# Stick-breaking attention: the triangular products of the suffix sums taken from two split parts of softplus

## The chip, the cores and the metric

One core of one Trainium2 chip runs the whole layer as one program. The metric is device time in microseconds (us), the median of three runs. Engines are named as in the profile: PE multiplies matrices (PEld is its weight load), DVE, ACT and POOL work on vectors, SP issues most of the DMAs.

## The reference

The layer has two attention groups side by side, an output projection, and a mixture of experts. The change is in the second group, stick-breaking attention, for 512 positions and 8 heads of 128 dimensions:

```python
def stick_breaking_block(q_blk, t_blk, k, v):
    s_pos = jnp.arange(k.shape[1], dtype=jnp.int32)
    strict = (s_pos[None, :] < t_blk[:, None])[None, None]
    z = jnp.einsum('bqhd,bshd->bhqs', q_blk, k).astype(jnp.float32)
    log_1m = jnp.where(strict, jax.nn.log_sigmoid(-z), 0.0)
    tail = lax.cumsum(log_1m, axis=3, reverse=True) - log_1m
    a = jnp.where(strict, jnp.exp(jax.nn.log_sigmoid(z) + tail), 0.0)
    return jnp.einsum('bhqs,bshd->bqhd', a.astype(v.dtype), v)
```

With log_sigmoid(-z) = -softplus(z) and log_sigmoid(z) = z - softplus(z), the weight of a position s is exp of z minus the sum of softplus over s and all later positions up to the query: a suffix sum of softplus along s.

## The kernel before

**Products.** Weights and activations of the big projections are held as two parts: a high part rounded to the type fp32r, and a low part, the float32 rest. Three products of 512 columns (`three`: high by high, high by low, low by high) replace one float32 product. In the attention stages the projections run as groups of six such products, named B (per-head projections, `main_b`) or Q (query projection, `main_q`) in the rows; these are the main products here. ACT rounds each weight chunk to its high part `hl`, and DVE subtracts to get the low part (`w_chunk`; POOL does it in a middle stretch).

**Stick-breaking.** The generator `stick(h)` does one head. Keys lie on the 128 partitions, queries on the free axis. Of each block of 128 keys only queries from that block on count, so the four key blocks have 512, 384, 256 and 128 columns. Three steps do them from the last keys to the first: blocks 3 and 2 together (256+128 = 384 columns), block 1 (384) and block 0 (512). Each step

- takes a PSUM bank `z` for the product of keys and queries (float32) and adds a strict causal mask;
- has ACT take |z|, exp and ln(1+...), and DVE (line 803) make softplus of it, in the tile `st` in SBUF, through the view `e`;
- adds onto `z`, on PE, the sums over all later key blocks (a product with `mones`, a matrix of minus ones, of the running column sums `tot`), and the suffix sum inside the block (a product with `negU`, which is the upper triangular matrix of ones minus one: only 0 and -1);
- keeps `tot` up to date on POOL;
- has ACT take exp of `z`, which gives the weights. `stick_pv` multiplies them with the values later.

The products with `mones` and `negU` are float32.

**What sets the order.** `tc.manual_schedule()` keeps the written order: each engine runs its instructions in the order in which the program issued them. Side work is written as generators in four lanes. `steps` runs the main products; after each group of six, `lanes.tick(rate)` advances lanes in turn, rate x 4 advances on average, and an advance runs a generator to its next `yield`. So what stands between two `yield` of `stick` is issued at once, and between one such piece and the next of the same head stand other lanes and, mostly, a group of main products. The rate is 1.2 (`RATES[0]`) while heads 0 to 3 run in two lanes, and 0.6 to 1.5 later. Heads 4 to 6 run at the same time in three lanes, head 7 behind them.

At the start of each main item `advance` issues the loads and the vector work of the weights: `w_chunk`, and `mod_chunk`, which sums the modulation's rows with one pass of DVE over 128x2048 per chunk (`gemv`, line 269, tile `accv`). These stand in DVE's queue between the passes of the heads. `norm_o` normalises group A beside the last blocks of heads 4 to 6: its passes are the rows Q, o00H, o00L, o01H and o01L.

**Pools.** Small tiles come from the pool `sm`, with rings by tag: "rb" has two buffers (among others the normalisation's `ro`), "tmp" three (`osq`, `rt`, `sqt`). A new tile of a ring waits until the tile that had its buffer has been read for the last time.

## Time and profile before

| | |
|---|---|
| median of three runs | 1876.78 us (1874.24 to 1879.22) |
| profiled execution, its own time | 1876.25 us |
| its span in the trace | 1874.4 us |
| mean granted clock of PE | 0.981 |
| busy: PE / DVE / ACT / POOL | 1735.2 / 938.9 / 507.6 / 153.2 us |
| stick-breaking's softplus passes on DVE | 24, between 248.8 and 668.5 us |

All times below come from the one profiled execution. A timeline row gives start, duration, engine, line, operation, what it writes and reads, and, in brackets, how long the engine was idle before it and what ended that. Ends of PE's products are modelled, so the start of the next product says more than a duration. A window row gives start and end, the length, the busy time of PE, PEld, DVE, ACT and POOL with their counts, the mean granted clock of PE, the DMA share and GB/s. Line 97 is the helper `act`, line 100 the helper `mm`, so go by tile names there. The mixture of experts, from about 700 us to the end, is bound by the DMAs of its weights.

### The profile page before, as it was taken

The page shows a single profiled execution, that of the slowest core. Times are in us where ns is not written, and L with a number is a line of the kernel's source. Part 1 is how long each engine was busy: PE and PEld are TensorE (multiplying, and loading weights), DVE is VectorE, ACT ScalarE, POOL GpSimd, SP SyncE. Part 2 cuts the span into 40 slices and gives each one's busy share as a digit, 9 for nine tenths or more (in the row PEclk, how much of TensorE's full clock was granted, in tenths as well). Part 3 has the DMA queues.
Part 4 walks back from the last instruction along what each step waited for, and adds up shares of the span by engine and source line. Part 5 has one row for each costly group of instructions (what it writes and reads, how often), then busy time and mean ns, then how long its engine had stood idle before and what let it go on. Part 6 is the DMA issues. An engine that isn't in the chain of part 4 may idle for free.

```text
span 1874.4 us, 20840 instructions
## 1 busy us (share of the span) xinstructions
PE 1735.2 (93%) x8097; PEld 975.6 (52%) x8097; DVE 938.9 (50%) x1518; ACT 507.6 (27%) x960; POOL 153.2 (8%) x116
## 2 busy tenths in 40 slices
PE   6999997999899998998899999999999999999997
PEld 3777775775567676887333333333333333333333
DVE  6798943378955857555334424342434233333425
ACT  4323342555455532321212111121112110211010
POOL 0001010332225110000100000000000000000000
PEclk8999998999999999999999999999999999999999
DMA  9876734312245645669899999999999999999997
GB/s 389 339 279 229 257 125 156 135 68 84 74 138 201 230 179 205 222 225 409 313 412 419 419 420 420 419 419 420 420 419 419 420 419 420 419 420 419 419 413 275
DMA packets 91574, 585.06 MB, mean 312 GB/s; under 512 B 10866, under 2 KB 11034, under 8 KB 27046
## 3 DMA queue, kind: packets, MB, share of 16 engines
q1 hardware_dynamic: 87184, 569.09, 76.0%
q0 software_dynamic: 4288, 14.60, 2.1%
q8 instruction: 65, 1.06, 0.2%
q14 instruction: 37, 0.30, 0.0%
HBM read 583.64 MB, written 8.40 MB: 316 GB/s over the span
## 4 chain that ended last, share of the span: by engine, by line
DMA 41%; PE 36%; DVE 14%; issue 4%; ACT 4%; POOL 1%; SPq 0%; DVEq 0%; ACTq 0%; POOLq 0%
DMA w_u<-in_w_up 15%; DMA w_g<-in_w_gate 12%; DMA w_d<-in_w_down 12%; PE O L100 8%; PE B L100 7%; PE y L100 3%; PE u L100 3%; PE Q L100 2%; PE g L100 2%; PE z L100 2%; DVE accv L269 2%; DVE acc L269 1%; PE cb L100 1%; DVE sel L722 1%; DMA w_m<-in_w_m 1%
## 5 line engine op out<-in xcount | busy, mean ns | idle before, releaser
L100 PE MATMUL u<-w_u,xe 128*64 128x512 f32 x1024 | 267.3, 605 | 22.8 <-DMA w_u<-in_w_up 21.6
L100 PE MATMUL g<-w_g,xe 128*64 128x512 f32 x1024 | 240.8, 596 | 18.2 <-DMA w_g<-in_w_gate 18.0
L1277 DVE TENSOR_TENSOR x<-cb,x 128x512 f32<-128x512 f32 x256 | 157.2, 681 | 186.2 <-PE cb L100 186.2
L100 PE MATMUL y<-w_d,uT 128*64 128x512 f32 x1024 | 236.9, 600 | 0.7 <-ACT uT L97 0.7
L100 PEld LDWEIGHTS u<-w_u,xe 128*64 128x64 f32 x1024 | 78.4, 138 | 200.9 <-issue 137.7
L100 PEld LDWEIGHTS g<-w_g,xe 128*64 128x64 f32 x1024 | 75.9, 137 | 170.5 <-issue 130.7
L269 DVE SCALAR_TENSOR_TENSOR accv<-w_m_None,sil,accv 128x2048 f32<-128x2048 f32 x62 | 150.4, 2426 | 6.7 <-DMA accv<-in_b_gate 6.5
L1267 DVE SCALAR_TENSOR_TENSOR yt<-y,gs,accv 128x512 f32<-128x512 f32 x64 | 47.8, 747 | 200.4 <-PE y L100 200.4
L97 ACT ACTIVATE xe<-ga,modc 128x128 f32<-128x128 f32 x254 | 93.9, 463 | 126.2 <-PE y L100 95.7
L100 PEld LDWEIGHTS y<-w_d,uT 128*64 128x64 f32 x1024 | 66.5, 136 | 116.0 <-issue 107.6
L100 PE MATMUL cb<-yH,oT 128*128 128x512 f32 x256 | 107.7, 421 | 0.9 <-DVE x L1277 0.9
L97 ACT ACTIVATE uT<-uT 128x512 f32<-128x512 f32 x16 | 9.6, 598 | 343.5 <-PE uT L1318 343.5
L100 PE MATMUL cb<-yL,oT 128*128 128x512 f32 x256 | 101.0, 394 | 0.0
L1269 DVE TENSOR_TENSOR yL<-yt,yH 128x512 fp32r<-128x512 f32 x64 | 44.3, 692 | 110.3 <-DMA w_g<-in_w_gate 52.7
L97 ACT ACTIVATE yH<-yt 128x512 fp32r<-128x512 f32 x64 | 40.3, 630 | 204.6 <-DVE yt L1267 121.4
L1219 POOL DMA_INDIRECT xg<-x1d,gi x15 | 15.2, 1014 | 818.7 <-DVE t L1222 597.2
L100 PEld LDWEIGHTS cb<-yH,oT 128*128 128x128 f32 x256 | 48.0, 188 | 49.8 <-issue 38.9
L1241 PEld LDWEIGHTS ga<-cst,xg 128*128 128x128 f32 x252 | 35.2, 209 | 62.9 <-issue 42.0
L97 ACT ACTIVATE hl<-w_B 128x1024 fp32r<-128x1024 f32 x48 | 50.5, 1052 | 54.9 <-DVE accv L269 29.5
L1312 DVE TENSOR_TENSOR u<-sg,u 128x512 f32<-128x512 f32 x16 | 11.0, 688 | 106.0 <-PE u L100 106.0
L381 DVE TENSOR_TENSOR hl<-w_O,hl 128x1024 fp32r<-128x1024 f32 x32 | 39.2, 1229 | 43.6 <-ACT hl L97 28.3
L381 POOL TENSOR_TENSOR hl<-w_B,hl 128x1024 fp32r<-128x1024 f32 x17 | 47.9, 2817 | 142.6 <-ACT hl L97 112.3
(428 smaller groups left out, 2915.4 us busy)
## 6 DMA issues: line engine op xcount, KB each, us to landing
w_g<-in_w_gate SPq DMA_DIRECT2D x128, 1024.0 KB, 19.9
w_u<-in_w_up SPq DMA_DIRECT2D x128, 1024.0 KB, 21.2
w_d<-in_w_down SPq DMA_DIRECT2D x128, 1024.0 KB, 19.9
w_m_None<-in_w_mod SPq DMA_DIRECT2D x64, 1024.0 KB, 4.9
w_m<-in_w_m SPq DMA_DIRECT2D x32, 1024.0 KB, 11.7
w_B<-in_w_b SPq DMA_DIRECT2D x48, 512.0 KB, 4.6
w_O<-in_w_o SPq DMA_DIRECT2D x16, 1024.0 KB, 5.0
w_A<-in_w_a SPq DMA_DIRECT2D x8, 848.0 KB, 11.3
```

The lines of the kernel that those rows point to most:

```text
L97: return SC.activation(o, i, f, **kw)
L100: return T.matmul(o, l, r, start=start, stop=stop, skip_group_check=skip)
L269: V.scalar_tensor_tensor(acc, w, s, acc, op0=OP.mult, op1=OP.add)
L381: low_eng[0].tensor_tensor(t[:, 1], s, t[:, 0].bitcast(F32), op=OP.subtract)
L722: V.match_replace(out=acc, in_to_replace=m8, in_values=acc, imm_value=SEL)
L1219: G.indirect_dma_start(xs, None, x1d[:, :], bass.IndirectOffsetOnAxis(ap=gi[:, 0:1], axis=0), bounds_check=S - 1, oob_is_err=False)
L1241: T.transpose(pb[:, 128 * j:128 * j + 128], xs[:, 512 * c:512 * c + 512].rearrange("p (k j) -> p j k", j=4)[:, j], ident)
L1267: V.scalar_tensor_tensor(yt, y, g, rowv[G2][:, cs], op0=OP.mult, op1=OP.mult)
L1269: V.tensor_tensor(yL[:, cs], yt, yH[:, cs].bitcast(F32), op=OP.subtract)
L1277: return lambda: V.tensor_tensor(acc[q][:, t], pb, acc[q][:, t], op=OP.add)
L1312: V.tensor_tensor(u, sg, pb, op=OP.mult)
```

## The change

`negU` gets the type fp32r; its values, 0 and -1, are the same in it. In each step of `stick` the products with `mones` stay as they were. Behind them two new tiles are made: `eH`, softplus rounded to fp32r by ACT, from the ring "rb"; and `eL` = softplus - eH, by DVE, from the ring "tmp". There is a `yield`; then `negU` is multiplied with eH and with eL, and the exponential is issued in the same piece. In the first step the addition on POOL is written ahead of the product with `mones`.

Per head that is three float32 steps of triangular products (four products, since the first step has two) replaced by eight products in fp32r, three more passes on ACT and three more on DVE. On ACT and DVE nothing else changes its place. `eL` is line 816, and lines behind it move by five.

```diff
@@ -132,7 +132,7 @@
     ones, mones = (t.to_broadcast([P, P]) for t in (one1, mone1))
     eps = sm.tile([P, 1], F32, name="eps")
     V.memset(eps, EPS)
-    negU = sm.tile([P, P], F32, name="negU")
+    negU = sm.tile([P, P], F32R, name="negU")
     cmask = cst[:, C_CM:C_CM + 128]
     ustrict = cst[:, C_US:C_US + 128]
     identb = sm.tile([P, P], BF, name="identb")
@@ -803,17 +803,22 @@
             V.scalar_tensor_tensor(e, z, 0.0, e, op0=OP.max, op1=OP.add)
             yield
             if js == (2, 3):
+                G.tensor_tensor(tot[:, 384:], e[:, 128:256], e[:, 256:384], op=OP.add)
                 mm(z[:, 128:256], mones, e[:, 256:384], False, False, True)
-                G.tensor_tensor(tot[:, 384:], e[:, 128:256], e[:, 256:384], op=OP.add)
             else:
                 mm(z[:, 128:], mones, tot[:, 128 * js[0] + 128:], False, False, True)
-            for j in js:
-                mm(z[:, at[j]], negU, e[:, at[j]], False, j == js[-1], True)
             if js == (1,):
                 G.tensor_tensor(tot[:, 256:], tot[:, 256:], e[:, 128:], op=OP.add)
             if js[0]:
                 G.tensor_copy(tot[:, 128 * js[0]:128 * js[0] + 128], e[:, 0:128])
-            yield
+            eH, eL = (sm.tile([P, S], F32R, name=n_, tag=t_, bufs=b_)[:, :n] for n_, t_, b_ in (("eH", "rb", 2), ("eL", "tmp", 3)))
+            act(eH, e)
+            V.tensor_tensor(eL, e, eH.bitcast(F32), op=OP.subtract)
+            yield
+            for j in js:
+                mm(z[:, at[j]], negU, eH[:, at[j]], False, False, True)
+            for j in js:
+                mm(z[:, at[j]], negU, eL[:, at[j]], False, j == js[-1], True)
             act(e, z, AF.Exp)
             yield
         weighed.append((h, buf))
```

DVE at head 3, middle and last block, before (`st<-z,st` is softplus, `accv` the modulation's sum, `hl` the low part of a weight chunk):

```order
L803 SCALAR_TENSOR_TENSOR st<-z,st 128x384
L269 SCALAR_TENSOR_TENSOR accv_2143<-w_m_None_2343,sil,accv_2143 128x2048
L381 TENSOR_TENSOR hl<-w_Q_2340,hl 128x1024
L803 SCALAR_TENSOR_TENSOR st<-z,st 128x512
L269 SCALAR_TENSOR_TENSOR accv_2143<-w_m_None_2408,sil,accv_2143 128x2048
L381 TENSOR_TENSOR hl<-w_Q_2450,hl 128x1024
```

The same place on DVE after the change:

```order
L803 SCALAR_TENSOR_TENSOR st<-z,st 128x384
L269 SCALAR_TENSOR_TENSOR accv_2184<-w_m_None_2391,sil,accv_2184 128x2048
L381 TENSOR_TENSOR hl<-w_Q_2388,hl 128x1024
L816 TENSOR_TENSOR eL<-st,eH 128x384
L803 SCALAR_TENSOR_TENSOR st<-z,st 128x512
L269 SCALAR_TENSOR_TENSOR accv_2184<-w_m_None_2458,sil,accv_2184 128x2048
L381 TENSOR_TENSOR hl<-w_Q_2504,hl 128x1024
L816 TENSOR_TENSOR eL<-st,eH 128x512
```

Each subtraction stands behind the modulation's pass and the weight split that follow the softplus it belongs to; nothing else moved.

PE at the middle block of head 3, before (Q is a main product):

```order
L100 MATMUL z<-st,mone_76 128x256
L100 MATMUL z<-st,negU 128x384
L100 MATMUL Q_2457<-cqsH,hl 128x512
L100 MATMUL Q_2457<-cqsL,hl 128x512
```

And after the change:

```order
L100 MATMUL z<-st,mone_76 128x256
L100 MATMUL z<-eH,negU 128x384
L100 MATMUL z<-eL,negU 128x384
L100 MATMUL Q_2511<-cqsH,hl 128x512
L100 MATMUL Q_2511<-cqsL,hl 128x512
```

Here the triangular products follow the sums without a main product between them, as before.

DVE at the first block of heads 4 to 6 (384 columns, three lanes), before:

```order
L803 SCALAR_TENSOR_TENSOR st<-z,st 128x384 x3
L267 TENSOR_SCALAR accv_4167<-w_m_None_4022,sil 128x2048
L269 SCALAR_TENSOR_TENSOR accv_4167<-w_m_None_4100,sil,accv_4167 128x2048
L381 TENSOR_TENSOR hl<-w_B_1_4103,hl 128x1024
L269 SCALAR_TENSOR_TENSOR accv_4167<-w_m_None_4165,sil,accv_4167 128x2048
L381 TENSOR_TENSOR hl<-w_B_1_4103,hl 128x1024
```

And after the change:

```order
L803 SCALAR_TENSOR_TENSOR st<-z,st 128x384 x3
L816 TENSOR_TENSOR eL<-st,eH 128x384 x2
L267 TENSOR_SCALAR accv_4235<-w_m_None_4086,sil 128x2048
L269 SCALAR_TENSOR_TENSOR accv_4235<-w_m_None_4164,sil,accv_4235 128x2048
L381 TENSOR_TENSOR hl<-w_B_1_4167,hl 128x1024
L816 TENSOR_TENSOR eL<-st,eH 128x384
L269 SCALAR_TENSOR_TENSOR accv_4235<-w_m_None_4233,sil,accv_4235 128x2048
L381 TENSOR_TENSOR hl<-w_B_1_4167,hl 128x1024
```

Two subtractions stand ahead of the two passes of the modulation and of the weight split, the third one behind them.

PE at the same block, second and third lane, before (B is a main product):

```order
L100 MATMUL z<-st,mone_76 128x128
L100 MATMUL z<-st,negU 128x256
L100 MATMUL z<-st,negU 128x128
L100 MATMUL z<-st,mone_76 128x128
L100 MATMUL z<-st,negU 128x256
L100 MATMUL z<-st,negU 128x128
L100 MATMUL B_4109<-hl,h0H 128x512 x2
L100 MATMUL B_4109<-hl,h0L 128x512
```

And after the change, where the triangular products of the first and of the second lane are seen:

```order
L100 MATMUL z<-st,mone_76 128x128
L100 MATMUL z<-eH,negU 128x256
L100 MATMUL z<-eH,negU 128x128
L100 MATMUL z<-eL,negU 128x256
L100 MATMUL z<-eL,negU 128x128
L100 MATMUL B_4174<-hl,h0H 128x512 x2
L100 MATMUL B_4174<-hl,h0L 128x512
L100 MATMUL B_4174<-hl,h0H 128x512 x2
L100 MATMUL B_4174<-hl,h0L 128x512
L100 MATMUL z<-eH,negU 128x256
L100 MATMUL z<-eH,negU 128x128
L100 MATMUL z<-eL,negU 128x256
```

The triangular products came directly behind their sums; now they follow a lane's advance later, with main products between, and a set is four products in place of two.

DVE at the last block of heads 4 to 6 (512 columns), before (Q and o01L are the normalisation):

```order
L803 SCALAR_TENSOR_TENSOR st<-z,st 128x512
L269 SCALAR_TENSOR_TENSOR accv_4167<-w_m_None_4294,sil,accv_4167 128x2048
L269 SCALAR_TENSOR_TENSOR accv_4167<-w_m_None_4349,sil,accv_4167 128x2048
L381 TENSOR_TENSOR hl<-w_B_3_4352,hl 128x1024
L888 SCALAR_TENSOR_TENSOR Q_2769<-Q_2769,vecs,ro_4307 128x512 x2
L892 TENSOR_TENSOR o01L<-Q_2769,o01H 128x512
L888 SCALAR_TENSOR_TENSOR Q_2769<-Q_2769,vecs,ro_4307 128x512
```

And after the change:

```order
L803 SCALAR_TENSOR_TENSOR st<-z,st 128x512
L816 TENSOR_TENSOR eL<-st,eH 128x512
L269 SCALAR_TENSOR_TENSOR accv_4235<-w_m_None_4382,sil,accv_4235 128x2048
L269 SCALAR_TENSOR_TENSOR accv_4235<-w_m_None_4446,sil,accv_4235 128x2048
L381 TENSOR_TENSOR hl<-w_B_3_4449,hl 128x1024
L816 TENSOR_TENSOR eL<-st,eH 128x512
L893 SCALAR_TENSOR_TENSOR Q_2833<-Q_2833,vecs,ro_4395 128x512 x2
L897 TENSOR_TENSOR o01L<-Q_2833,o01H 128x512
L893 SCALAR_TENSOR_TENSOR Q_2833<-Q_2833,vecs,ro_4395 128x512
L897 TENSOR_TENSOR o01L<-Q_2833,o01H 128x512
L816 TENSOR_TENSOR eL<-st,eH 128x512
```

The first lane's subtraction is ahead of the long passes, the second lane's behind them, and the third lane's five passes of the normalisation later.

PE at the same block, from the second lane's sums on, before:

```order
L100 MATMUL z<-st,mone_76 128x384
L100 MATMUL z<-st,negU 128x512
L100 MATMUL z<-st,mone_76 128x384
L100 MATMUL z<-st,negU 128x512
L100 MATMUL B_4110<-hl,h2H 128x512 x2
```

And after the change:

```order
L100 MATMUL z<-st,mone_76 128x384 x2
L100 MATMUL B_4174<-hl,h2H 128x512 x2
L100 MATMUL B_4174<-hl,h2L 128x512
L100 MATMUL B_4174<-hl,h2H 128x512 x2
L100 MATMUL B_4174<-hl,h2L 128x512
L100 MATMUL z<-eH,negU 128x512
L100 MATMUL z<-eL,negU 128x512
L100 MATMUL z<-eH,negU 128x512
L100 MATMUL z<-eL,negU 128x512
```

The sums of the second and the third lane now stand together, then a group of main products, and then the triangular products of the first two lanes.

## Rows read from the trace of the kernel before

**Rows 1.** The page: shares of the chain that ended last, by engine

```profile
DMA 41%; PE 36%; DVE 14%; issue 4%; ACT 4%; POOL 1%; SPq 0%; DVEq 0%; ACTq 0%; POOLq 0%
```

**Rows 2.** Windows: start:end, length, busy of PE, PEld, DVE, ACT, POOL, clock, DMA

```profile
330.00:370.00 40.00, 39.78 (x171) 28.98 (x171) 15.51 (x14) 22.28 (x38) 13.23 (x11) 1.00 0.40 140
...
395.00:440.00 45.00, 42.41 (x197) 30.04 (x195) 38.83 (x96) 24.60 (x57) 11.84 (x6) 0.96 0.21 71
```

**Rows 3.** Timeline of PE: start us, duration us, what, count

```profile
264.19 1.02 PE L100 MATMUL z<-B,B 128*128 128x512 f32 x2
...
265.05 0.22 PE L100 MATMUL z<-smaskb,identb 128*128 128x128 bf16 x1
...
598.26 5.49 PE B L100 x24
...
103.08 0.27 PE L100 MATMUL nat<-waH,h1H 128*128 128x208 f32 x1
...
103.19 0.27 PE L100 MATMUL nat<-waL,h1H 128*128 128x208 f32 x1
```

**Rows 4.** Groups of the page and of one tile (count: lowest/median/highest ns)

```profile
L1269 DVE TENSOR_TENSOR yL<-yt,yH 128x512 fp32r<-128x512 f32 x64 | 44.3, 692 | 110.3 <-DMA w_g<-in_w_gate 52.7
...
L97 ACT ACTIVATE yH<-yt 128x512 fp32r<-128x512 f32 x64 | 40.3, 630 | 204.6 <-DVE yt L1267 121.4
...
L97 ACT ACTIVATE st<-st x24: 523/526/632, 247.6 to 666.3; 128x384 f32<-128x384 f32 x16, 128x512 f32<-128x512 f32 x8
...
L803 DVE SCALAR_TENSOR_TENSOR st<-z,st x24: 547/558/693, 248.8 to 667.8; 128x384 f32<-128x384 f32 x16, 128x512 f32<-128x512 f32 x8
```

**Rows 5.** Timeline of DVE and PE, middle block of head 3

```profile
346.67 2.34 DVE L269 SCALAR_TENSOR_TENSOR accv<-w_m_None,sil,accv 128x2048 f32<-128x2048 f32 x1
...
346.90 0.67 PE L100 MATMUL z<-st,mone 128*128 128x256 f32 x2 [0.22 <-DVE st L803]
...
350.13 1.22 DVE L381 TENSOR_TENSOR hl<-w_Q,hl 128x1024 fp32r<-128x1024 f32 x1 [1.12 <-ACT hl L97]
```

**Rows 6.** Timeline of PE and DVE, heads 4 to 6, first block

```profile
583.21 0.38 PE L100 MATMUL z<-st,mone 128*128 128x128 f32 x2
...
585.30 3.28 DVE L269 SCALAR_TENSOR_TENSOR accv<-w_m_None,sil,accv 128x2048 f32<-128x2048 f32 x1
...
595.33 1.12 PE L100 MATMUL md<-accv,one 128*128 128x512 f32 x2 [1.59 <-ACT st L97]
```

**Rows 7.** Timeline of DVE and PE, heads 4 to 6, last block

```profile
627.97 4.73 DVE L269 SCALAR_TENSOR_TENSOR accv<-w_m_None,sil,accv 128x2048 f32<-128x2048 f32 x2
...
630.07 1.02 PE L100 MATMUL z<-st,negU 128*128 128x512 f32 x2
...
632.62 1.22 DVE L381 TENSOR_TENSOR hl<-w_B,hl 128x1024 fp32r<-128x1024 f32 x1
...
642.94 0.50 PE L100 MATMUL B<-hl,h3H 128*128 128x512 f32 x1 [1.14 <-DVE hl L381]
```

**Rows 8.** Windows and timeline of PE behind longer waits

```profile
290.70:296.00 5.30, 5.21 (x12) 3.81 (x12) 0.00 (x0) 0.00 (x0) 3.21 (x4) 0.51 0.00 0
...
688.70:692.00 3.30, 3.23 (x8) 2.59 (x9) 3.23 (x6) 0.00 (x0) 0.00 (x0) 0.52 0.24 99
...
290.79 1.19 PE L100 MATMUL z<-st,mone 128*128 128x256 f32 x2 [3.79 <-DVE st L803]
...
688.77 1.19 PE L100 MATMUL O<-hl,o00H 128*128 128x512 f32 x2 [3.38 <-DVE mix L1013]
...
303.70 0.88 PE L100 MATMUL z<-st,mone 128*128 128x384 f32 x2 [2.64 <-DVE st L803]
```

**Rows 9.** Timeline of POOL, and of DVE beside it, head 0

```profile
249.50 0.45 POOL L807 TENSOR_TENSOR st<-st 128x128 f32<-128x128 f32 x1 [54.97 <-DVE st L803]
...
251.01 2.49 POOL L807 TENSOR_TENSOR st<-st 128x128 f32<-128x128 f32 x1 [0.83 <-DVE st L803]
...
250.85 2.34 DVE L269 SCALAR_TENSOR_TENSOR accv<-w_m_None,sil,accv 128x2048 f32<-128x2048 f32 x1
```

## The prediction

> **What bounds the kernel now.** I read the page first: in the chain that ended last DMA has 41%, PE 36%, DVE 14% [rows 1]. The DMA share is the stage of the experts. Everything before it has an order written out by hand, so that stage starts when the attention stages are done, and a microsecond lost or won there comes through to the end. So what counts is how long PE's queue takes through the stretches where the eight heads of stick-breaking run: about 246 to 357 us for heads 0 to 3 and 575 to 673 for heads 4 to 7 (the first and the last softplus passes stand in [rows 4]). In the window of head 3 PE is busy 39.78 of 40 us, and DVE and ACT only 15.5 and 22.3 [rows 2]: what PE saves there is time, if nothing else comes late. Then I read the same stretches as a timeline, engine by engine, and asked of each new instruction what stands ahead of it in its engine's queue.
>
> **What the products save.** One head has three blocks; their triangular products have 256+128, 384 and 512 columns. Today each is a float32 product: a float32 product of 512 columns holds PE from 264.19 to 265.05, 0.86 us, so 0.64 for 384 columns. Products of split parts run already in this kernel: 24 of 512 columns take 5.49 us, 0.23 each, and with 208 columns they start 0.11 us apart [rows 3]. The two new products of a part pair cost 2 x 0.23 = 0.46 for 512 columns (0.40 saved), about 0.35 for 384 (0.29 saved), and 4 x 0.11 = 0.45 for 256+128 (0.19 saved; I take 0.11 for 128 columns too, bounds 0.06 by columns and 0.11 by that row). Sum: 0.88 a head, **7.0 us for eight heads**. The products with the matrix of minus ones stay float32 and cost what they cost.
>
> **What is added.** 24 rounding copies on ACT and 24 subtractions on DVE. The nearest rows: a copy into fp32r of 128x512 takes 0.63 us, the subtraction behind it 0.69; for 384 columns an ACT pass over the same tile takes 0.53 and a DVE pass with two inputs 0.56 [rows 4]. That is 13 us on ACT and 14 us on DVE, engines with room. It is their latency that counts: a subtraction can be done 0.53+0.56, with hand-over about 1.3 us, after the softplus is. PE has cover for it: between the sums and the triangular products the order now puts six main products, 1.37 us by the 24 in 5.49 [rows 3]. At 18 of the 24 places the order has the subtraction right behind the softplus on DVE (or one step behind), and I cost those at nothing. If that cover were gone, each would cost up to 1.3.
>
> **Where the subtraction is not right behind.** DVE takes its queue in order, and at six places something long stands ahead of eL. PE waits there with everything behind it.
>
> Head 3, middle block: ahead of eL stand the gemv of the modulation and the weight split hl. In the trace the sums start on PE at 346.90 and end about 0.43 later. The gemv runs 346.67 to 349.01; then ACT copies the weights, and DVE's half of the split, released by that copy, runs 350.13 to 351.35 [rows 5]. ACT's rounding copy stands behind the weight copy (350.1 to 350.6), and eL behind the split: 351.35 + 0.56 = 351.9. The order leaves no main product between sums and triangular product here, so PE waits from 347.33 to 351.9: **4.6**. In the last block of this head the same two stand ahead; I let that eat its gain: **0.4**.
>
> Heads 4 to 6, first block, three lanes at once. eL of the third lane stands behind two other eL, a gemv pair, and the split. Before, the gemv ended at 585.30+3.28 = 588.58 [rows 6]; the split starts 1.12 behind it, as in [rows 5]. Two subtractions and their wait for ACT move the gemv by about 1.65, to 590.2; split 591.4 to 592.6; third eL done at 593.1. PE, from 583.2 on, has two sums (0.43), a group of six (1.37), a sum (0.21), a first set of products (0.45), a group, a second set: it stands before the third set from 587.5. Behind the wait come a group, two blocks of z (0.7 each), a group, one more z: 598.3. In the trace PE came to that point at 595.33, after a wait of 1.59 [rows 6]. So the block ends 3.0 later though its products save 0.57: **3.6** of waits. In the middle block an eL again follows two gemvs, but there PE has two more float32 products and waits in any case; I let it eat 0.5 of the gain of 0.87: **0.5**.
>
> Heads 4 to 6, last block. Here eH comes from a pool of two buffers of which the normalisation of group A holds one, so the second lane's copy waits until PE has read the first lane's, and the third's until PE has read the second's. On DVE, the second eL stands behind two gemvs and a split. In the trace that trio starts at 627.97 and ends at 632.62+1.22 = 633.84 [rows 7]; the extra subtractions of the middle and the last block (0.56+0.69) put it at about 635.2, and eL at 635.9. At 630.07 PE has the sums of this block behind it [rows 7]; a group (1.37) and the first lane's products (0.46) later, at 631.9, PE is there: 4.0. The third eL then stands behind five passes of the output split (0.7 each: 639.3), and its copy behind ACT's copy for the last of them, so that it is done at about 640.8; PE, after one group, is there at 637.6: 3.2. The softplus comes 0.8 later too, and the 1.14 that PE now waits at 642.94 [rows 7] goes: **6.9**. The products of head 7 have clean places.
>
> **The clock.** After a wait of 3.79 us PE's granted clock was 0.51 from 290.7 to 296.0, and after one of 3.38 us 0.52 from 688.7 to 692; after one of 2.64 us the next product of 384 columns took no longer than elsewhere [rows 8]. Half speed for 5.3 us loses 2.6, for 3 us 1.5; I take 2.0 for head 3, 2.0 for the first block, and 1.0 for the last block, where slow products use up part of the next wait: **5.0**, bounds 0 and 8. Another 0.5 of gain in heads 0 to 2 I give to a wait that is there anyway (the one before 303.70 [rows 8]).
>
> **Sum:** -7.0 + 0.5 + 4.6 + 0.4 + 3.6 + 0.5 + 6.9 + 5.0 = +14.5. On the profiled execution's 1876.25 us (its span is 1874.4; the median of the runs is 1876.78, so it is a typical one) that is **1890.7 us**.
>
> **POOL and DVE.** POOL's 128x128 addition took 0.45 us at 249.50 and 2.49 at 251.01, the second while DVE ran a gemv [rows 9]. [...]
>
> **Rivals.** (a) POOL holds DVE up: if each new subtraction in the three-lane blocks waits for POOL's running operation, the first block's gemv starts up to 0.9 later (half of 2.49 less the 0.69 of its own), and POOL's copies, which ACT's exponentials wait for, come about 1 later (half of 2.49 less 0.45) [rows 4, 9]: 16.4, so 1892.7. It needs POOL busy at the moment of eL, which it is in the first block only. (b) **Faster:** the cover holds. If eL is done within about 1.6 us of the start of the sums at every place, no wait is added and the 7.0 stay: 1869. For it: 18 of 24 places are clean. Against it: at the six others, the instructions ahead are there in the order, with durations from the trace. It decides at one place, head 3's middle block: if PE waits there for less than 1 us, this is the case. (c) **No change:** the lateness is taken back. From 395 us on, DVE sets the pace (38.8 of 45 us busy [rows 2]), and if its queue there doesn't start later, the 4.0 net of heads 0 to 3 (-3.5+0.5+4.6+0.4+2.0) go; if PE's clock also stays up in heads 4 to 6 (3.0) and the wait of 3.38 at 688.7 shrinks by as much as PE is late, 14.5-4.0-3.0-3.4 = 4.1: 1880.4. Against it: the index products that start DVE's work there stand behind the late ones on PE. (d) The new products are no faster than float32: then 2 x 0.86 for 0.86, +17.1 in place of -7.0, 1914.8; the 0.23 of [rows 3] speak against it.
>
> **How the numbers follow.** A measurement here can tell about 0.3%, 5.6 us, from no change. Forecast 0.62, (a) 0.15, (c) 0.13, (b) 0.08, (d) 0.02. Slower by over 0.3% holds the first two and (d): 0.79; within 0.3%: 0.13; faster: 0.08. The range goes down into (c), to 1877, and up past (a) with the clock term at its upper bound, to 1900; it leaves out (b), (d) and the edges of the others.
>
> **What would show it.** In the profile after: the triangular products at 0.23 us for 512 columns; PE waiting for eL on DVE at head 3 for over 4 us, and twice for over 3 us in heads 4 to 6; a granted clock near 0.5 behind those waits; the start of the experts' stage later by some 14 us. If the sum of PE's waits for DVE at z is below 5 us, I am wrong in the places; if they are there and the end is no later, I am wrong in what follows them.

## The result, and the profile after

The change makes the kernel slower: 1896.07 us (median of 6 runs, 1893.14 to 1904.23) against 1877.63, a ratio of 1.0101 with a 95% interval of 1.0081 to 1.0122. That is 18.4 us, or 1.0%; the prediction was 1890.7, and 1877 to 1900. The six runs spread over 11 us, more than those of the kernel before (1874.24 to 1879.96), and the mean granted clock goes with the time: 0.976 in the run of 1893.61, 0.972 in that of 1904.23. The profiled execution is the slowest of the six, so its trace shows some 8 us more than the median.

First the chain of the page, which answers to [rows 1]; it is followed back less far than before (68% of the span in place of 100%), so its shares say little here.

```profile
DMA 41%; PE 20%; DVE 4%; issue 2%; ACT 1%; POOL 0%; SPq 0%; DVEq 0%; POOLq 0%; ACTq 0%
```

The products, as [rows 3]. The timeline of PE in heads 0 and 1, 512 columns (start, duration, what):

```profile
273.20 0.40 PE L100 MATMUL z<-eH,negU 128*128 128x512 f32 x1
...
273.44 0.39 PE L100 MATMUL z<-eL,negU 128*128 128x512 f32 x1
...
273.67 0.40 PE L100 MATMUL z<-eH,negU 128*128 128x512 f32 x1
```

They start 0.23 us apart, 0.47 for a pair, as forecast. The new passes, as [rows 4], by tile (count: lowest/median/highest ns):

```profile
L97 ACT ACTIVATE eH<-st x24: 506/524/630, 251.0 to 696.4; 128x384 fp32r<-128x384 f32 x16, 128x512 fp32r<-128x512 f32 x8
...
L816 DVE TENSOR_TENSOR eL<-st,eH x24: 548/682/1336, 251.6 to 697.7; 128x384 fp32r<-128x384 f32 x16, 128x512 fp32r<-128x512 f32 x8
```

Head 3, middle block, as [rows 5], timeline of DVE, ACT and PE (the brackets: idle before, and what ended it):

```profile
349.60 2.34 DVE L269 SCALAR_TENSOR_TENSOR accv<-w_m_None,sil,accv 128x2048 f32<-128x2048 f32 x1
...
349.82 0.67 PE L100 MATMUL z<-st,mone 128*128 128x256 f32 x2 [0.23 <-DVE st L803]
...
352.93 0.51 ACT L97 ACTIVATE eH<-st 128x384 fp32r<-128x384 f32 x1
...
353.06 1.23 DVE L381 TENSOR_TENSOR hl<-w_Q,hl 128x1024 fp32r<-128x1024 f32 x1 [1.12 <-ACT hl L97]
...
353.49 0.44 PE L100 MATMUL z<-eH,negU 128*128 128x384 f32 x1 [3.00 <-ACT eH L97]
...
354.20 0.55 DVE L816 TENSOR_TENSOR eL<-st,eH 128x384 fp32r<-128x384 f32 x1
...
354.81 0.69 PE L100 MATMUL z<-eL,negU 128*128 128x384 f32 x1 [0.87 <-DVE eL L816]
```

The softplus is done ahead of 349.60, but eH starts at 352.93, behind the weight copy that waits for the modulation (349.60 to 351.94), and eL at 354.20, behind the weight split. PE, done with the sums at 350.25, waits 3.00 for eH and 0.87 for eL: 3.9.

Heads 4 to 6, first block, as [rows 6]:

```profile
599.40 2.07 DVE L816 TENSOR_TENSOR eL<-st,eH 128x384 fp32r<-128x384 f32 x2 [0.39 <-ACT eH L97]
...
602.73 2.43 DVE L269 SCALAR_TENSOR_TENSOR accv<-w_m_None,sil,accv 128x2048 f32<-128x2048 f32 x1
...
606.16 0.51 ACT L97 ACTIVATE eH<-st 128x384 fp32r<-128x384 f32 x1
...
606.72 0.44 PE L100 MATMUL z<-eH,negU 128*128 128x256 f32 x2 [3.64 <-ACT eH L97]
...
607.54 0.81 DVE L816 TENSOR_TENSOR eL<-st,eH 128x384 fp32r<-128x384 f32 x1
...
608.40 0.69 PE L100 MATMUL z<-eL,negU 128*128 128x256 f32 x2 [1.24 <-DVE eL L816]
```

The third lane's eH and eL stand behind the modulation, the weight copy and the split; PE waits 3.64 and 1.24. Last block, as [rows 7]:

```profile
649.66 4.73 DVE L269 SCALAR_TENSOR_TENSOR accv<-w_m_None,sil,accv 128x2048 f32<-128x2048 f32 x2
...
651.83 0.63 ACT L97 ACTIVATE eH<-st 128x512 fp32r<-128x512 f32 x1 [2.54 <-PE z L100]
...
652.51 0.50 PE L100 MATMUL z<-eH,negU 128*128 128x512 f32 x1 [0.48 <-ACT eH L97]
...
654.31 1.22 DVE L381 TENSOR_TENSOR hl<-w_B,hl 128x1024 fp32r<-128x1024 f32 x1
...
655.45 0.69 DVE L816 TENSOR_TENSOR eL<-st,eH 128x512 fp32r<-128x512 f32 x1
...
656.19 0.80 PE L100 MATMUL z<-eL,negU 128*128 128x512 f32 x1 [3.18 <-DVE eL L816]
...
660.08 0.79 PE L100 MATMUL z<-eH,negU 128*128 128x512 f32 x1 [0.54 <-ACT eH L97]
```

The second lane's copy waits for PE to read the first lane's (2.54 on ACT), its eL waits for the two modulation passes and the split, and PE waits 0.48 for the copy and 3.18 for eL; the third lane costs it 0.54. Together 4.2.

PE's clock, as [rows 8], in windows of the trace (length, busy us of PE, PEld, DVE, ACT, POOL with counts, then granted clock, DMA share, GB/s):

```profile
304.50:311.20 6.70, 6.70 (x47) 5.35 (x42) 2.91 (x5) 0.00 (x0) 0.00 (x0) 0.56 0.38 128
...
355.60:359.00 3.40, 3.40 (x10) 2.25 (x10) 0.00 (x0) 0.48 (x1) 0.00 (x0) 0.63 0.69 277
...
396.60:403.40 6.80, 6.80 (x23) 5.67 (x22) 2.90 (x11) 2.40 (x5) 1.79 (x1) 0.57 0.00 0
...
486.00:500.00 14.00, 10.18 (x36) 7.49 (x35) 13.45 (x22) 4.62 (x9) 2.39 (x1) 0.76 0.22 75
...
608.30:615.00 6.70, 6.60 (x17) 4.44 (x18) 2.34 (x2) 1.01 (x2) 4.74 (x3) 0.56 0.48 159
...
656.10:666.30 10.20, 9.57 (x25) 6.75 (x26) 9.24 (x12) 6.17 (x11) 0.00 (x0) 0.55 0.37 132
```

In five of them the granted clock is 0.55 to 0.63. Three of the five stand right behind the three long waits; the one at 304.5 stands behind a wait for softplus at 302.87 that has grown from the 2.64 of [rows 8] to 3.77, and the one at 396.6 behind no wait that the timeline of PE shows. The window from 486 has such a part too, 6 us at 0.50 (492 to 498); the kernel before has 4 us at 0.56 and 0.58 (480 to 484; 0.88 from 478 to 492). So the forecast's three places are not all. Over the whole span the granted clock is 0.972 of 1902.5 us, in place of 0.981 of 1874.4; the share that was not granted makes 53 us in place of 36, so by this estimate the lower clock can have cost up to 18 us in the profiled execution.

To see where the time went, I took seven ACT instructions that stand in every kernel, at 209, 340, 376, 575, 618, 656 and 718 us in the kernel before, and compared their starts. A row says how many us a stretch takes more than in the kernel before, by the profiled executions; the last row comes from the spans. e1 is the changed kernel once more; the other experiments follow. By their times the profiled executions of after (1904.23), e1 (1901.59) and e6 (1878.60) stand 6 to 8 us above the medians of their kernels, and that of e4 (1896.09) at it. From 209 to 718 us e10 repeats the column of e1 and e5 that of e9, to 0.1 in each row.

```
stretch of before (us)        after    e1    e2    e3    e4    e6    e7    e9
up to 209                       0.7   0.1  -0.7  -0.4   0.3   0.4   1.4   0.4
209-340  heads 0 to 2           3.3   3.3   5.3   0.0   1.0  -0.8   0.7   3.2
340-376  head 3                 4.7   4.7   0.6   0.0   5.5  -1.2   0.1   3.2
376-575  indexer, group A       6.2   6.2   3.3   1.2   1.3   2.4  -0.1   1.3
575-618  heads 4-6, blocks 1,2  6.2   6.2   5.5   0.0   5.9  -2.8  -0.3   3.5
618-656  heads 4-6, block 3     7.0   7.0   6.9   0.1   7.0   1.1   5.1   6.5
656-718  head 7                -0.7  -0.6  -0.7  -0.6   0.0  -1.1   0.0  -0.7
718-end  output, experts        0.7  -1.6   0.1   0.3  -1.1   4.4   2.4  -1.1
```

### The profile page after: what moved, and what is told of

The parts are those of the page before. It is cut to its first block, busy times and chain, and to the rows that moved or that the text cites. A ratio compares the mean times of both kernels' runs of the same rounds, so it can differ in the third digit from the quotient of the medians.

```text
span 1902.5 us, 20883 instructions
## 1 busy us (share of the span) xinstructions
PE 1746.8 (92%) x8097; PEld 986.3 (52%) x8097; DVE 954.7 (50%) x1542; ACT 519.4 (27%) x984; POOL 141.9 (7%) x116
## 4 chain that ended last, share of the span: by engine, by line
DMA 41%; PE 20%; DVE 4%; issue 2%; ACT 1%; POOL 0%; SPq 0%; DVEq 0%; POOLq 0%; ACTq 0%
DMA w_u<-in_w_up 15%; DMA w_g<-in_w_gate 13%; DMA w_d<-in_w_down 13%; PE O L100 8%; PE y L100 3%; PE u L100 2%; PE g L100 2%; PE B L100 1%; PE cb L100 1%; PE z L100 1%; DVE x L1282 1%; PE router L100 1%; ACT st L97 1%; DMA xg<-x1d,gi 1%; DVE accv L269 0%
## 5 line engine op out<-in xcount | busy, mean ns | idle before, releaser
L381 DVE TENSOR_TENSOR hl<-w_B,hl 128x1024 fp32r<-128x1024 f32 x31 | 39.1, 1262 | 37.4 <-ACT hl L97 37.4
## 6 DMA issues: line engine op xcount, KB each, us to landing
w_g<-in_w_gate SPq DMA_DIRECT2D x128, 1024.0 KB, 19.9
w_d<-in_w_down SPq DMA_DIRECT2D x128, 1024.0 KB, 19.9
```

The source lines that it names most:

```text
L381: low_eng[0].tensor_tensor(t[:, 1], s, t[:, 0].bitcast(F32), op=OP.subtract)
```

## The experiments

Theory A, the prediction's: six subtractions reach PE late, and the clock falls behind those waits. B: the clock falls at times of its own. C: the added passes cost at all 24 places. Two came on the way. D: in heads 0 to 2 and 7 other waits take what PE saves, and in heads 4 to 6 DVE's queue is nearly full. F: a gain in the experts' stage comes from where the load buffers begin; G, against it, that the filling products of e5 gave all of e5's gain. Diffs are against the changed kernel, those of e7, e11 and e12 against the kernel before.

### e1_again: the changed kernel, unedited

> The changed kernel once more, unedited, beside the three below. Theory A (six subtractions reach PE late because of what stands ahead of them in the queues of DVE and ACT, and PE's clock falls behind those waits): 1893 to 1904 us, with the same waits of PE at the triangular products, about 4 us in head 3, 5 in the first block of heads 4 to 6 and 4 in the last block, since they come from the order. Theory B (the clock falls at times of its own, whatever PE waits for): the waits stay, but the stretches at half clock lie elsewhere and the time moves with them. Theory C (the added passes themselves cost, through ACT, DVE and POOL, at all 24 places): the time is the same and waits are spread over many places.

Measured: 1895.51 us (4 runs, 1894.02 to 1901.59), ratio 1.0091 (1.0065 to 1.0118). The waits are those of after, to a tenth: PE waited for eH 7.6 us in four waits, for eL 6.2 in six, for softplus 9.0. So the waits come from the order. The profiled run (1901.59) has the stretches of after at a lower clock as well (0.58 to 0.71 where after has 0.55 to 0.63), shifted by the 0.6 us by which it starts earlier.

### e2_split_early: the split ahead of the yield

```diff
             V.scalar_tensor_tensor(e, z, 0.0, e, op0=OP.max, op1=OP.add)
+            eH, eL = (...)
+            act(eH, e)
+            V.tensor_tensor(eL, e, eH.bitcast(F32), op=OP.subtract)
             yield
...
-            eH, eL = (...)
-            act(eH, e)
-            V.tensor_tensor(eL, e, eH.bitcast(F32), op=OP.subtract)
-            yield
             for j in js:
                 mm(z[:, at[j]], negU, eH[:, at[j]], False, False, True)
...
+            yield
             act(e, z, AF.Exp)
```

> The rounding copy and the subtraction are written directly behind the softplus pass, ahead of the yield, and the split products directly behind the sums, with the exponential one piece later, as in the kernel before. The passes are the same 48. Theory A: nothing long stands ahead of a subtraction any more, PE waits for one at most about 1 us at a place, the three long waits go, 1870 to 1884 us. Theory C: the same passes cost the same, 1890 us or more. Theory B says nothing on the waits.

Measured: 1897.0 us (4 runs, 1895.37 to 1898.17), ratio 1.0102 (1.0075 to 1.0128). A's time fails and C's "1890 us or more" is met, though the waits go as A says: for eL 3.3 us in 13 waits, none over 0.6, and head 3 costs 0.6 in place of 4.7. But the last block of heads 4 to 6 costs 6.9 as before. DVE and PE there:

```profile
640.78 0.69 DVE L806 TENSOR_TENSOR eL<-st,eH 128x512 fp32r<-128x512 f32 x1 [1.91 <-ACT eH L97]
...
646.93 0.69 DVE L806 TENSOR_TENSOR eL<-st,eH 128x512 fp32r<-128x512 f32 x1 [0.76 <-ACT eH L97]
...
661.25 1.22 DVE L381 TENSOR_TENSOR hl<-w_B,hl 128x1024 fp32r<-128x1024 f32 x1
...
659.82 0.51 PE L100 MATMUL B<-hl,h3H 128*128 128x512 f32 x1 [0.87 <-ACT hl L97]
...
662.52 0.72 PE L100 MATMUL B<-hl,h3H 128*128 128x512 f32 x1 [2.19 <-DVE hl L381]
```

Each subtraction now holds DVE still until ACT has made its eH (1.91, 0.76, 0.76 us idle, and 0.7 of work; ahead of the first eH three other passes stand on ACT). All that stands behind it comes that much later: the weight split ends at 662.47, and PE waits 0.87 and 2.19 for weights where it waited 1.14 [rows 7]. The wait has moved from the subtraction to the weights. This is theory D for this block: DVE's queue is full there (22.5 of 25 us busy from 625 to 650 in the kernel before, as the windows below show), and whatever is added to it comes out on PE. The first blocks still cost 5.5 and heads 0 to 2 cost 5.3, and a full queue does not explain these: from 600 to 625 us PE is busy 19.86 us in place of 23.79 while DVE is busy only 12.28. PE's idle time there is in waits of under 1.5 us each, nearly all of them for ACT. What makes them was not taken apart.

### e3_heads_0127 and e4_heads_3456: the change by halves

```diff
+            if not (h in (0, 1, 2, 7)):        # e4: (3, 4, 5, 6)
+                for j in js:
+                    mm(z[:, at[j]], negU.bitcast(F32), e[:, at[j]], False, j == js[-1], True)
+                yield
+            else:
                 eH, eL = (...)
...
```

> The change in heads 0, 1, 2 and 7 alone, whose subtractions stand right behind the softplus; heads 3 to 6 as before. Theory A: four times 0.88 us is saved and no long wait is added, 1872 to 1877 us. Theory C: half of the loss stays, about 1887.

> The change in heads 3 to 6 alone, the heads with the six late places; heads 0, 1, 2 and 7 as before. Theory A: nearly the whole loss, 1892 to 1902 us, with the three long waits. Theory C: half of the loss, about 1887.

Measured: e3 1877.49 us (10 runs), ratio 1.0002 (0.9990 to 1.0013); e4 1896.17 us (4 runs), ratio 1.0102 (1.0076 to 1.0129). The whole loss sits in heads 3 to 6, which speaks against C. But the 3.5 us that e3 saves on PE do not come through either. It is 3.5 us ahead at 300 us (the sums that started at 303.70 [rows 8] start at 300.16), 1.5 of it won since 246, and only 0.4 ahead at 325, as much as it was at 209. In between, windows of e3 and then of before:

```profile
301.10:307.80 6.70, 6.70 (x81) 5.06 (x80) 3.21 (x6) 0.00 (x0) 0.00 (x0) 0.61 0.24 66
...
314.70:321.40 6.70, 6.70 (x20) 5.27 (x19) 5.58 (x3) 1.06 (x1) 0.00 (x0) 0.61 0.49 163
```

```profile
301.10:307.80 6.70, 4.10 (x74) 2.88 (x75) 2.91 (x7) 1.66 (x3) 0.00 (x0) 1.00 0.48 159
...
314.70:321.40 6.70, 5.94 (x19) 4.55 (x19) 5.51 (x8) 1.21 (x2) 0.00 (x0) 0.75 0.70 260
```

In the first window before ran at full clock, e3 at 0.61; in the second 0.75 and 0.61. PE did its work faster, and what it saved went into running the next products at 0.61.

### e5_fill and e9_fill_alone: PE kept at work in the three waits

```diff
+    zero1 = sm.tile([P, 1], F32, name="zero1")      # e9: a second column of the tile of eps
+    V.memset(zero1, 0.0)
+    zeros = zero1.to_broadcast([P, P])
...
             yield
+            for _ in range({(3, 1): 6, (3, 0): 0, (6, 2): 7, (5, 0): 4}.get((h, js[0]), 0)):
+                mm(z, zeros, one1.to_broadcast([P, n]), False, False, True)
```

> The changed kernel, with float32 products of a zero matrix added onto z just ahead of the late triangular products: 6 of 384 columns in head 3's middle block, 7 of 384 in head 6's first block, 4 of 512 in head 5's last block, 3.4 to 4.5 us of work each, about what PE waits there. They add zero. Theory A (PE's clock falls because it waits): the waits are filled, the half-clock stretches behind them (355 to 359, 608 to 615 and 656 to 666 us in the changed kernel) go, and half their 20 us comes back: 1884 to 1892 us. Theory B (the clock falls at times of its own): these stretches stay, 1895 to 1902 us.

> The changed kernel with the same filling products of zeros as e5_fill, but the zero column lies in a tile that was there, so that no buffer moves by the 32 bytes that e5_fill's new tile took. In e5_fill the start of the experts' stage came 11 us earlier than in e1_again, and 16 us more were won after it, where the weights came at 426 GB/s in place of 419. Theory F (the filling kept PE's clock up and gave the 11 us; the 32 bytes gave the 16 us): 1884 to 1888 us, 419 GB/s. Theory G (the filling gave all): 1875 us, 426 GB/s.

Measured: e5 1875.45 us (10 runs, 1873.16 to 1878.65), ratio 0.9996 (0.9987 to 1.0006), far below every expectation. Its trace reached the instruction at 718 us 11 us earlier than e1's and won 15 more behind that, where nothing was edited (16 against the kernel before); its weights came at 426 GB/s. Its new tile of 32 bytes had moved every buffer behind it. So e9 repeats it without moving anything: 1891.56 us (6 runs, 1890.11 to 1894.99), ratio 1.0068 (1.0042 to 1.0094), 3.6 us above the range of F, far above G's 1875, with F's 419 GB/s. It is 4 us under e1 by the medians (their intervals overlap) and 9 by the profiled runs. The same pair with the buffers moved is e5 and e10 (below): 1875.45 and 1881.07, 5.6 us apart, and there too the intervals overlap. Windows of e9:

```profile
355.50:358.90 3.40, 3.40 (x16) 2.36 (x15) 0.00 (x0) 1.68 (x3) 0.00 (x0) 1.00 0.64 263
...
396.60:403.40 6.80, 6.80 (x30) 4.30 (x29) 4.70 (x16) 3.81 (x7) 2.87 (x3) 1.00 0.01 2
...
486.00:500.00 14.00, 12.70 (x47) 9.11 (x47) 12.99 (x29) 6.14 (x15) 2.39 (x1) 0.88 0.30 94
...
608.30:615.00 6.70, 6.40 (x26) 4.98 (x27) 2.27 (x3) 5.36 (x11) 0.00 (x0) 1.00 0.94 342
...
652.70:656.00 3.30, 3.30 (x14) 2.67 (x13) 3.08 (x3) 1.67 (x3) 0.00 (x0) 0.72 0.19 37
...
656.10:666.20 10.10, 10.10 (x48) 8.39 (x47) 4.14 (x4) 3.43 (x7) 1.22 (x3) 1.00 0.86 328
```

The four stretches from 355.6 on that had 0.55 to 0.63 have 1.00 now, the window from 486 has 0.88 in place of 0.76, and no run is above 1895. In the last block a shorter fall is left, at 652.7 with 0.72, behind a wait of 2.0 us for the third lane's eH, which is not filled, and the one at 304.5 is still there (0.61). So it is PE's idle time that sets off the falls behind the three long waits here (A): 0.63, 0.56 and 0.55 in after, 1.00 with the waits filled. That filling it with products that do nothing pays is likely, by two pairs of medians that point the same way, but their intervals overlap. By the table e9 takes 1.5 us less than e1 in head 3 (4.7 to 3.2), 2.7 in the first blocks of heads 4 to 6, 0.5 in the last block, and 4.9 between 376 and 575, where no filling stands. The first three make 4.7, about what the medians gain; the 4.9 seem to come only in executions above the median. The fall at 396 is in after, e1, e2 and e10 (0.57, 0.61, 0.63 and 0.61) and not in before, e3, e4, e5 and e9 (1.00 each); e4 has the long waits of head 3 and not the fall, e2 the fall without the waits. What sets it off stays open (B is not excluded there).

### e6_high_only: the faster products by themselves

```diff
-            V.scalar_tensor_tensor(e, z, 0.0, e, op0=OP.max, op1=OP.add)
+            eH = sm.tile([P, S], F32R, name="eH", tag="tmp", bufs=3)[:, :n]
+            V.scalar_tensor_tensor(eH, z, 0.0, e, op0=OP.max, op1=OP.add)
...
+                mm(z[:, at[j]], negU, eH[:, at[j]], False, j == js[-1], True)
```

> The products' saving by itself: the softplus pass writes fp32r directly, one fp32r product takes the place of each float32 one, right behind the sums; no rounding copy, no subtraction. It leaves out the low part of softplus, so its weights are a little off. PE does 1.52 us less a head, 12.2 in all. Theory A (PE sets the pace in all eight heads): 1863 to 1867 us. Theory D (formed after the runs before: in heads 0 to 2 and 7 other waits end last and take the gain, and in heads 4 to 6 DVE's queue is nearly full): less than half of it comes through, 1870 to 1876 us.

Measured: 1871.62 us (10 runs, 1868.38 to 1878.60), ratio 0.9967 (0.9956 to 0.9979). Of 12.2 us less work on PE 5 to 6 come through, as D has it. With no copy and no subtraction at all, a microsecond saved on PE was worth about half of one here.

### e7_passes_unused: the added passes by themselves

```diff
             for j in js:
                 mm(z[:, at[j]], negU, e[:, at[j]], False, j == js[-1], True)
...
+            eH, eL = (...)
+            act(eH, e)
+            V.tensor_tensor(eL, e, eH.bitcast(F32), op=OP.subtract)
             yield
```

> The kernel before with the 24 rounding copies and 24 subtractions at the places that the changed kernel gives them, but nothing reads them: the products are the float32 ones of before, right behind the sums. PE waits for none of the new passes. Theory A: no wait, 1875 to 1880 us. Theory D: in heads 4 to 6 the passes move the modulation and the weight split back on DVE's queue, and PE waits for the weights: 1880 to 1888 us.

Measured: 1885.61 us (4 runs, 1884.41 to 1885.63), ratio 1.0047 (1.0031 to 1.0064): nearly 9 us for passes that nobody reads, as D has it. By the table 5.1 of the 9.3 in the profiled run are in the last block of heads 4 to 6, none in head 3 and in the first blocks; 3.8 lie ahead of 209 and behind 718, where nothing was edited. What made these 3.8 is not known, so the passes account for 5 to 9 us. In the last block DVE does one subtraction more ahead of the two modulation passes, one behind the split and one among the passes of the normalisation, and PE waits for weights again:

```profile
640.70 0.69 DVE L818 TENSOR_TENSOR eL<-st,eH 128x512 fp32r<-128x512 f32 x1 [0.62 <-ACT eH L97]
...
644.21 0.50 PE L100 MATMUL B<-hl,h3H 128*128 128x512 f32 x1 [0.92 <-ACT hl L97]
...
646.90 0.79 PE L100 MATMUL B<-hl,h3H 128*128 128x512 f32 x1 [2.19 <-DVE hl L381]
```

0.92 and 2.19 in place of the 1.14 before. How full DVE is, in windows of before and of e7:

```profile
625.00:650.00 25.00, 23.86 (x99) 17.57 (x99) 22.50 (x21) 11.76 (x21) 5.33 (x3) 1.00 0.47 175
```

```profile
625.00:650.00 25.00, 21.37 (x81) 15.31 (x80) 21.43 (x25) 12.66 (x22) 1.21 (x3) 0.93 0.45 169
```

In before DVE is busy 22.50 of the 25 us; PE, busy 23.86, has just enough weights. In e7 PE loses 2.5 us of its busy time there; DVE's own busy time falls too, by its waits for eH (0.62 at 640.70, and 3.17 behind the split). The new tiles share their rings with the normalisation, which could have been held up by that instead; but from 575 to 665 us only eL, eH and the passes on softplus wait for them in this trace, and no pass of the normalisation.

### e8_sub_on_pool: the subtractions on POOL

```diff
-            V.tensor_tensor(eL, e, eH.bitcast(F32), op=OP.subtract)
+            G.tensor_tensor(eL, e, eH.bitcast(F32), op=OP.subtract)
```

> The changed kernel with the 24 subtractions on POOL, so that they stand behind nothing on DVE and DVE's queue is the one of before; the rounding copies stay on ACT at their places. Theory A: the waits for eL behind the modulation go, but each of the POOL passes takes about 1.4 us and more, and head 3's copy still stands behind ACT's weight copy: 1884 to 1894 us. Theory D: the last block of heads 4 to 6 costs no more than 3 us in place of 7. Theory C (passes on POOL shut DVE out): 1896 us or more.

Measured: 1927.1 us (4 runs, 1926.69 to 1927.86), ratio 1.0271 (1.0254 to 1.0289), far above A's range; D fails too, since the last block of heads 4 to 6 takes 9 us more. The subtraction by tile, and PE's largest waits (us in total, times, longest):

```profile
L816 POOL TENSOR_TENSOR eL<-st,eH x24: 984/1022/3342, 250.5 to 717.1; 128x384 fp32r<-128x384 f32 x16, 128x512 fp32r<-128x512 f32 x8
...
PE z L100 <- POOL eL L816: 26.2, 16, 4.5
```

A pass takes POOL from 1.0 to 3.3 us. It stands in one queue with the running sums, and PE waits for it at 16 places, 26.2 us. POOL had room by its busy share, but not in time. C's "1896 or more" is met. What it names, DVE slower beside POOL, the trace of the kernel before shows at four weight splits: those that begin on DVE at 186.49, 263.70, 340.02 and 679.81 us, with POOL at work beside them, took 1.81 and three times 1.48 us where the median is 1.22. How much of the loss in e8 comes from it was not separated, and the run can't say what DVE's queue costs with the subtractions off it.

### e10_moved_32, e11_before_moved_32, e12_before_moved_96: buffers moved

```diff
+    pad = sm.tile([P, 8], F32, name="pad")          # e12: [P, 24]
+    V.memset(pad, 0.0)
     eps = sm.tile([P, 1], F32, name="eps")
```

> The changed kernel with a tile of 32 bytes per partition that nothing reads, written ahead of the other tiles, so that the buffers that the weights are loaded into lie 32 bytes further. Theory F: the weights of the experts come at 426 GB/s, 1878 to 1882 us, with the waits and the half-clock stretches of the changed kernel. Theory G: 1895 us, 419 GB/s.

> The kernel before with the same tile of 32 bytes. Theory F: 426 GB/s in the experts' stage, 1860 to 1863 us, faster than both kernels. Theory G: 1877 us.

> The kernel before with a tile of 96 bytes. Moved by 32 the buffers start at a multiple of 256 bytes, moved by 96 at a multiple of 64 alone. If 64 is enough: 426 GB/s and the time of e11_before_moved_32. If it takes 256: 419 GB/s, 1877 us.

Measured: e10 1881.07 us (10 runs, 1876.32 to 1887.98), ratio 1.0010 (0.9988 to 1.0031); e11 1861.99 us (5 runs, 1861.44 to 1863.50), ratio 0.9916 (0.9888 to 0.9944); e12 1873.22 us (10 runs), ratio 0.9984 (0.9964 to 1.0004). Windows of 800 us in the experts' stage, of before, e11 and e12 (the last number is GB/s):

```profile
1000.00:1800.00 800.00, 755.23 (x3206) 292.00 (x3204) 278.82 (x510) 125.71 (x287) 12.96 (x13) 1.00 1.01 419
```

```profile
1000.00:1800.00 800.00, 757.69 (x3253) 310.83 (x3250) 284.37 (x521) 128.25 (x292) 12.98 (x13) 0.99 1.01 426
```

```profile
1000.00:1800.00 800.00, 754.85 (x3218) 298.00 (x3216) 278.08 (x509) 128.24 (x294) 12.98 (x13) 1.00 1.01 421
```

419, 426 and 421 GB/s at a DMA share of 1.01 each time. After and e9, whose buffers stand as before, show 419 in this window too, and e5, e10 and e11, moved by 32, show 426. A load of `w_g` took a median of 19.9 us from issue to landing in before, 19.6 in e11 and 19.8 in e12. 1.7% of the some 900 us that the experts take is 15 us, which is what e11 gains on before and e10 on e1 (14.4). So F holds for the place of the buffers, which all moved together, though it put the filling at 11 us: by the medians the filling gave 4 to 6 and the 32 bytes the rest of e5's 20. e12's time can't be told from before; its rate is neither of the two that were expected, but nearer to the one of before. The kernel before with 32 unused bytes is the fastest version here, 15 us under the kernel it came from and 34 under the changed one.

## Why the prediction was right, and where it was not

The sign, the time (5.4 us off) and the places were right. That the number came so near is in part luck: head 3 was put 1.4 too high and the first blocks of heads 4 to 6 1.5 too low, and in the last block waits that were put 3.0 too high stood in for a cost that the sum did not have.

- **What the products save** was right in size (0.47 us a pair of 512 columns) and wrong in worth. The step "what PE saves there is time" failed: of e6's 12.2 us about half came through, of e3's 3.5 nothing. It was read from one window, that of head 3 [rows 2], where PE is always busy; in heads 0 to 2 of e3 the saved time went into stretches at a clock of 0.61, and the term of 0.5 for a wait that is there anyway should have been all of their 2.6. With the change in all heads that stretch even costs 3.3 (e1), with the change in heads 0, 1, 2 and 7 alone nothing (e3). Windows of before and of after show the clock there:

```profile
300.00:345.00 45.00, 38.20 (x272) 28.28 (x271) 17.72 (x19) 16.67 (x29) 6.29 (x4) 0.96 0.47 164
```

```profile
300.00:345.00 45.00, 37.97 (x254) 28.10 (x255) 17.99 (x21) 14.86 (x26) 3.26 (x4) 0.85 0.48 164
```

- **Head 3, middle block:** 4.6 forecast, 3.9 measured, through the very instructions that were named. The sign that was named, a wait of over 4 us for eL on DVE, is not met as written: 3.00 of it is for eH, behind ACT's weight copy, and 0.87 for eL. From the end of the sums (350.25) to eL's product (354.81) it is 4.6, with eH's product in it, which the sum had put behind the wait. The last block's 0.4 is 0.40 in the trace. Net of the savings and with the clock the sum had 6.1 for this head; the table has 4.7.
- **Heads 4 to 6, first blocks:** 3.6 and 0.5, with 2.0 for the clock and 1.4 saved, is 4.7 net; the table shows 6.2, and 3.5 with the clock kept up. PE waits 4.9 before the third set.
- **Heads 4 to 6, last block:** 6.7 net forecast, 7.0 measured, but the mechanism was only half of it. The waits for eH and eL are 4.2, not 7.2. e2 took the lateness away and kept the 6.9, and e7 has 5.1 without PE reading the passes: here DVE's queue is the bound, and a subtraction costs where it stands, early or late. (No run took the subtractions off DVE without adding waits elsewhere; e6, which has none, costs 1.1 here.) The step "engines with room" failed; it too was read from head 3's window, while DVE's share in this block is 22.5 of 25.
- **The clock:** 5.0 forecast behind the waits; e9 against e1 gives 1.5 + 2.7 + 0.5 = 4.7, for the 2.0, 2.0 and 1.0 of the sum. Not forecast: 6.2 more between 376 and 575 in the profiled runs, 4.9 of which go with the filling. These probably come and go between executions: e4, profiled at its median, has 1.3 there, and the granted clock of after's runs goes with their time.
- **The rivals.** (a) POOL against DVE: passes of DVE are longer beside POOL, on top of the forecast's places; no run shows that one waits for the whole of POOL's running operation, as (a) has it. The first two subtractions of the three-lane block take 2.07 us in a row, where two at the lowest of the tile's row take 1.1, with POOL at work beside them all the time; that is the 0.9 of (a) on the modulation. The third has 0.81 in place of 0.55, with POOL beside it too. The further 1 us on POOL's copies was not separated, and the time of (a), 1892.7, is nearer to the measured one than 1890.7. (b) Its point of decision, a wait of under 1 us in head 3's middle block, failed with 3.9. (c) The lateness isn't taken back from 395 us on: the stretch adds time. (d) The products are as fast as forecast, 0.23 us for 512 columns.

By place the profiled execution of e4, which stands at its median, has 5.5 + 5.9 + 7.0 = 18.4 of its 19.9 us in head 3 and in the two parts of heads 4 to 6, where the forecast had 17.5. The start of the last stage, forecast some 14 us later, is 21 us later in e4 and 27 in the profiled execution of after. What lies between 14.5 and the 18.4 of the median of after is mostly the missing gain in heads 0 to 2 (3.3 in place of the forecast -2.1, by the profiled executions); a part can be the clock between 376 and 575. How much each is in an execution at the median can't be told from traces of executions above it.

## What to carry to other kernels

Put a price on a new pass by the busy share of its engine in that very stretch, not in a neighbouring one: behind the queue that was 90% full here it cost its length and its waits, wherever it was placed. What a saturated PE saves is worth something only if the next wait behind it doesn't take it, and a longer wait can bring a lower clock, which takes more: here 5 to 6 of 12.2 us came through in e6, and the clock was 0.55 to 0.63 behind waits of 3.7 to 4.9 us. Before tuning microseconds in the middle of a program whose end is bound by its loads (419 GB/s at a DMA share of 1.01), look at where its buffers begin: here 32 bytes were worth 15 us, where the whole change cost 18.

## What the runs showed of the hardware that was not expected

- **The loads ran faster with the buffers 32 bytes further on.** In the built programs the weight buffers of both kernels start 32 bytes short of a multiple of 256. Moved by 32 bytes, to a multiple of 256, the same transfers run at 426 GB/s; moved by 96, to 64 past a multiple of 256, at 421; unmoved at 419. That is 1.7% and 0.5% more than unmoved. The unused tile moves everything behind it, so that the load buffers were not moved alone, and why the rate changes no run shows.
- **Products of zeros kept the clock up.** With 17 float32 products of zeros in three waits the clock was 1.00 (e9) in windows where it was 0.55 to 0.63 (after). The medians are 4 to 6 us lower, with intervals that overlap.
- **A subtraction on POOL** of 384 or 512 columns took between 0.98 and 3.34 us; on DVE they took a median of 0.68, and up to 1.34 with POOL at work beside them.
